# Hymba step on one core: four of the nine token-square sums as a multiply-and-sum on VectorE, their task spawned later

## The chip, the cores and the metric

The kernel runs on one core of a Trainium2 chip. The metric is the device time of one execution in microseconds (us), as the median of the runs shown. The names of the engines are those of the profile: PE is TensorE's matmuls, PEld its weight loads, DVE is VectorE, ACT is ScalarE, POOL is GpSimd, and SP is SyncE, which here only issues DMAs. A queue of DMA issues on an engine is written SPq or ACTq.

## The reference

One layer is computed for 1024 prompt tokens and 32 sample tokens (T = 1056 columns in all, model width 1024). Both branches read the same normalised input through one input projection; the outputs of both are gated and go through one output projection.

```python
def _rmsnorm(x, g):
    y = xf * lax.rsqrt(jnp.mean(xf * xf, axis=-1, keepdims=True) + EPS) * g
...
hn = _rmsnorm(x, ln_g)
q, k, v, ga, u, gs = jnp.split(hn @ w_in, [...])
att = stick_breaking(q, k, v)                 # 8 heads x 64, strictly causal
...
ab = exp(a * dt); bb = (ab - 1) / a * b       # complex, 32 groups x 64 states
h = scan(ab, bb @ u); y = gelu(c @ h + d_skip * u)
ssm_y = y * sigmoid(y @ w_glu + b_glu)
...
out = concat[_rmsnorm(att) * silu(ga), _rmsnorm(ssm_y) * silu(gs)] @ w_out
return x + out, k, v, h_last                  # then a last _rmsnorm
```

The mean of xf * xf over the 1024 columns of each token is what the change is about: nine blocks of up to 128 tokens, one sum per token.

## The kernel before, in words

**Products.** fp32 matrices are split into a high and a low part, and each product is made of three matmuls: high x high (`xh,w_hi`), low x high (`xl,w_hi`), high x low (`xh,w_lo`). I call these three a triple. ACT writes the high part of a weight (`w_hi`), DVE or POOL the low one (`w_lo`). The x that is multiplied is not yet normalised: the reciprocal root `rsc` of each token is worked out beside, spread over all partitions by PE (`tr<-ident,rsc`) and copied to `rsx`, by which every projected tile is scaled when it leaves PSUM.

**Order of the projections.** The 1056 tokens are cut into 256, 384 and 416. `slot(i, ...)` works through one group of 128 output columns in 24 steps (8 slices of the contraction x 3 cuts). Slot 0 makes two groups of u while the inputs arrive; then come the other groups of u, the gate groups (`gs`), the first attention gate (`ga`, stored as `tga_d`), q, k and v. PE's matmuls of the slots fill the time in which the state-space branch waits for other engines.

**The state-space branch.** `angles` and `params_d` make sines, cosines (tables `RT`), step parameters (`P`) and the powers of the step (`PW`); `s_mats(m)` makes from them the matrices `W` (written `W<-Pm,Bm`, `tW`), which PE transposes. u is stored scaled to DRAM (`ud`) and read back as `U`. `s_states(m)` runs the scans (`E<-dec,E`) on DVE, up to `bst`; `s_out(m)` makes Y on PE in two halves (`z<-U,Tm` and `z<-bst,V`) of which ACT takes the gelu out of PSUM, writes Y to DRAM (`yd`) and reads it back turned (`yj`). When all four m are there, ACT and DVE split y (`yh`, `yl`) and `glu` makes the products with `w_glu` (`z<-yh,wgh` and so on) for the three cuts. Behind the last of these `ssm_gate` loads the gate (`gs<-gs_d`), multiplies on DVE, takes its sigmoid on ACT (`sgs`) and multiplies on POOL (`y_nat<-y_nat,sgs`), for m = 0 to 3; two buffers hold the gates, so those of m = 2 and 3 are loaded when the first two are used up. The attention starts at the first `z<-kA,qA`.

**What sets the order.** Every call on an engine goes through the helper `Timed.call` (line 215, so that all rows of the profile bear this line). The helper keeps an estimated clock for each engine (class `Clock`, l. 72 to 150). `spawn` puts a task, a Python generator, on a list; `tick`, called at each step of a slot, goes on with each task whose data are ready by the estimated clock (`at`, `dve`) or that was named as done. An engine runs its instructions in the order in which they were so issued. A task that is issued elsewhere, or priced otherwise, therefore moves other tasks' instructions too.

**The square task.** `x_rs` (l. 386) takes the nine blocks in turn. Block 8 has 32 tokens and shares its buffer with block 0, so its load is issued once block 0 is squared. `x_sq` (l. 377) squares a block in place on ACT with the sum in `rst`; then come six small operations on POOL (`rsqrt`), the transposes on PE and the copies to `rsx`. The task is spawned at step `RSS % 24` of slot `RSS // 24`, `angles` and `params_d` at that of `PST`, which is 34 (slot 1, step 10).

Of the kernel before, what the change touches and what calls it, by code (L numbers as in the profile page):

```python
# [12 lines left out]
AF = mybir.ActivationFunctionType  # L13
OP = mybir.AluOpType
# [10 lines left out]
NCH = 133  # L25
NB = 134
NK = 25
RSS = 28
LEAD = 1
WARM = 9  # L30
WL = {1: ((1, slice(0, 1)),), 2: ((0, slice(1, 3)), (1, slice(1, 3))), 4: ((0, slice(3, 8)),), 5: ((1, slice(3, 8)),)}
# [188 lines left out]
def hymba_step(ctx, tc, xT, xn, w_in, ln_g, kcT, vc, w_glu, b_glu, w_out, g_att, g_ssm, final_g,  # L220
               prm, h0, bmat, cvec, cbd, dsk, consts_in,
               y_out, kT_out, vT_out, st_out):
    nc = Clock(tc.nc)
# [153 lines left out]
    def x_sq(b):  # L377

        m, _ = blk(b)
        nc.scalar.activation(xq[b][:m], xq[b][:m], AF.Square, accum_out=rst[:m, 1, b:b + 1])  # L380

    xq = {}
    rsc = const.tile([128, 9], F32, name="rsc")
    rst = const.tile([128, 2, 9], F32, name="rst")

    def x_rs():

        for b in range(9):
            if b == 1:
                x_load(8)  # L390
            yield at(xq[b], lead=300.0)
            x_sq(b)
        rsqrt(rsc, rst[:, 1], 1.0 / D, rst[:, 0], rst[:, 1])
        yield at(rsc)
        for i, (t0, n) in enumerate(TC):
            pb = p_tr()
            for b in range(t0 // 128, (t0 + n + 127) // 128):
                m, c = blk(b)
                nc.tensor.matmul(pb[:, c.start - t0:c.stop - t0], rsc[:m, b:b + 1].to_broadcast([m, 128]),
                                 ident[:m, :m], start=True, stop=True)  # L400
            act(rsx[:, t0:t0 + n], pb[:, :n])
            done.add(f"rs{i}")
            yield 3 if i == 0 else 1

    def blk(b):
        return min(128, T - 128 * b), slice(128 * b, min(T, 128 * b + 128))
# [336 lines left out]
    with ExitStack() as s1:  # L743
# [100 lines left out]
        def angles():  # L844

            u = ss.tile([128, 16, NK], F32, name="ang_u", tag="E")
            v = sa.tile([128, 16, NK], F32, name="ang_v", tag="W")
            sb = [128, 16, NK]
            kb = kidx[:, None, :].to_broadcast(sb)
            yield "pa"  # L850
            tt(v, kb, p8[:, :, None].to_broadcast(sb), OP.mult)
            yield dve()
            ts(v, v, MAGIC, MAGIC, OP.add, OP.subtract)
            yield dve()
            tt(u, kb, ph[:, :, None].to_broadcast(sb), OP.mult)
            yield dve()
            tt(u, u, v, OP.subtract)
            yield dve()
            tt(v, kb, pl[:, :, None].to_broadcast(sb), OP.mult)
            yield dve()  # L860
            tt(u, u, v, OP.add)
            yield dve()
            ts(u, u, 0.5, -0.5, OP.min, OP.max)
            yield dve()
            sincos(RT[:, 1], RT[:, 0], u, v)
            params_b()
            done.add("pb")
            yield 2
            params_c()
            done.add("pc")  # L870
# [279 lines left out]
        def at_step(slot, k, f, *a):  # L1150
            ev.setdefault((slot, k), []).append((f, a))
# [8 lines left out]

        at_step(RSS // 24, RSS % 24, spawn, x_rs())
        at_step(PST // 24, PST % 24, spawn, angles())
# [905 lines left out]
```

## Time and profile before

| | |
|---|---|
| median of 3 runs | 681.17 us (680.73 to 681.33) |
| the profiled execution | 682.8 us |
| its span in the trace | 680.9 us |
| mean granted clock of TensorE | 0.968 |
| PE busy | 626.7 us (92%) |
| DVE busy | 429.1 us (63%) |
| ACT busy | 346.3 us (51%) |
| POOL busy | 228.1 us (33%) |

The span is what the trace covers, from its first to its last instruction; the time of the execution is 1.9 us more. All times inside the kernel are us from the start of the span. A row of a timeline gives start, length, engine, operation, output and inputs, and in brackets the idle time before it with what ended it. [...]

### The profile page before, as it was taken

To read this page: it belongs to the slowest core of one execution; us is meant where nothing else is said; L and a number is where in the kernel's file an instruction comes from. 1 tells how busy PE (TensorE), PEld (TensorE's weight loads), DVE (VectorE), ACT (ScalarE), POOL (GpSimd) and SP (SyncE) were. 2 spreads that over 40 slices of the span, in tenths; PEclk is the share of its full clock that TensorE was granted. 3 is DMA by queue.
4 is the path that set the end of the run, shared out by engine and by line. 5 is a ranking of instruction groups with operands and counts; after the bars stand their busy time and mean duration, and the time that the engine had idled before them with its cause. 6 is when DMAs were issued, how large, how long until landed. Compare 5 with 4: busy or idle time off the path is not lost.

```text
span 680.9 us, 10474 instructions
## 1 busy us (share of the span) xinstructions
PE 626.7 (92%) x3760; PEld 523.9 (77%) x3760; DVE 429.1 (63%) x670; ACT 346.3 (51%) x787; POOL 228.1 (33%) x334
## 2 busy tenths in 40 slices
PE   7948999999969993899999999999998899997995
PEld 6938899988969993788878698886775566756873
DVE  5947999889335443465776565656557948364654
ACT  5572423252555643566766657555765645442332
POOL 0011122000122167444345343432417513133885
PEclk7969999999979996999999999999999999998999
DMA  8726342552520144210221112333162795218552
GB/s 307 270 90 175 95 143 79 178 167 66 177 69 24 56 166 153 67 36 25 64 87 59 46 44 74 95 103 102 39 184 92 254 286 178 69 63 269 182 172 100
DMA packets 64132, 83.46 MB, mean 123 GB/s; under 512 B 9040, under 2 KB 47248, under 8 KB 64080
## 3 DMA queue, kind: packets, MB, share of 16 engines
q1 hardware_dynamic: 57600, 71.23, 32.4%
q10 hardware_dynamic: 6480, 11.56, 5.4%
q8 instruction: 30, 0.49, 0.3%
q14 instruction: 22, 0.18, 0.1%
HBM read 56.29 MB, written 26.48 MB: 122 GB/s over the span
## 4 chain that ended last, share of the span: by engine, by line
PE 69%; POOL 6%; DMA 5%; ACT 4%; issue 3%; DVE 3%; SPq 1%; DVEq 0%; POOLq 0%; ACTq 0%
PE pj L215 36%; PE z L215 14%; PE pv L215 10%; PE tr L215 8%; POOL rst L215 2%; DMA gs<-gs_d 1%; DMA x<-in_xn 1%; POOL rsA L215 1%; DMA w_raw<-in_w_in 1%; DMA yj<-yd 1%; DVE cb L215 1%; DMA yd<-Y 1%; SPq L215 1%; POOL s__6538 L215 0%; DMA O<-att_d 0%
## 5 line engine op out<-in xcount | busy, mean ns | idle before, releaser
L215 PE MATMUL pj<-xh,w_hi 128*128 128x256 f32 (+2 forms) x472 | 163.9, 350 | 0.0
L215 PE MATMUL pj<-xl,w_hi 128*128 128x256 f32 (+2 forms) x472 | 151.4, 324 | 0.0
L215 PE MATMUL pj<-xh,w_lo 128*128 128x256 f32 (+2 forms) x472 | 151.3, 323 | 0.0
L215 PEld LDWEIGHTS pj<-xh,w_hi 128*128 128x128 f32 x472 | 89.9, 190 | 23.7 <-issue 19.8
L215 DVE TENSOR_TENSOR_SCAN cb<-cb,own 128x896 f32<-128x896 f32 (+3 forms) x64 | 96.5, 1514 | 15.0 <-ACT cb L215 12.8
L215 PEld LDWEIGHTS pj<-xl,w_hi 128*128 128x128 f32 x472 | 90.2, 191 | 1.7
L215 PEld LDWEIGHTS pj<-xh,w_lo 128*128 128x128 f32 x472 | 89.5, 190 | 0.3
L215 ACT ACTIVATE cb<-z 128x512 f32<-128x512 f32 (+4 forms) x102 | 49.8, 488 | 53.0 <-PE z L215 34.7
L215 PE MATMUL pj<-xh,S 128*128 128x512 f32 (+3 forms) x212 | 69.4, 405 | 2.1 <-DVE x L215 1.5
L215 POOL TENSOR_TENSOR betaL<-betaL,cb 128x896 f32<-128x896 f32 (+2 forms) x24 | 41.4, 1725 | 60.8 <-DVE cb L215 36.9
L215 POOL TENSOR_TENSOR w_lo<-w_raw,w_hi 128x512 fp32r<-128x512 f32 x30 | 46.5, 1550 | 44.3 <-ACT w_hi L215 44.3
L215 ACT ACTIVATE wt<-tr 128x512 f32<-128x512 f32 (+2 forms) x86 | 47.2, 552 | 16.6 <-PE tr L215 16.3
L215 PE MATMUL pv<-wt,vS 128*64 128x256 f32 x320 | 52.0, 404 | 1.1 <-POOL wt L215 1.1
L215 POOL TENSOR_TENSOR betaS<-betaS,cb 128x128 f32<-128x128 f32 (+3 forms) x32 | 27.1, 851 | 73.2 <-DVE cb L215 38.3
L215 PEld LDWEIGHTS pj<-xh,S 128*128 128x128 f32 (+2 forms) x212 | 36.2, 184 | 17.2 <-issue 7.5
L215 DVE TENSOR_TENSOR kv_out<-pj,rsx 128x256 f32<-128x256 f32 (+2 forms) x55 | 28.3, 514 | 29.5 <-PE pj L215 29.0
L215 PE MATMUL pj<-xl,S 128*128 128x512 f32 (+3 forms) x112 | 43.1, 387 | 0.0
L215 ACT ACTIVATE w_hi<-w_raw 128x512 fp32r<-128x512 f32 x44 | 27.6, 630 | 27.0 <-DMA w_raw<-in_w_in 17.0
L215 PE MATMUL tr<-ident,betaL 128*128 128x128 f32 x226 | 35.8, 276 | 4.1 <-ACT wt L215 2.6
L215 ACT ACTIVATE betaL<-z 128x512 f32<-128x512 f32 (+4 forms) x70 | 35.8, 512 | 0.0
L215 PEld LDWEIGHTS tr<-ident,betaL 128*128 128x128 f32 x226 | 26.9, 141 | 11.1 <-ACT wt L215 3.4
L215 DVE TENSOR_TENSOR attT<-pv,attT 64x256 f32<-64x256 f32 x32 | 13.4, 420 | 32.6 <-ACT attT L215 32.4
(273 smaller groups left out, 1273.3 us busy)
## 6 DMA issues: line engine op xcount, KB each, us to landing
w_raw<-in_w_in ACTq DMA_DIRECT2D x44, 256.0 KB, 2.6
xq<-in_xn SPq DMA_DIRECT2D x8, 512.0 KB, 7.4
x<-in_xn SPq DMA_DIRECT2D x8, 512.0 KB, 5.7
yp_d<-x SPq DMA_DIRECT2D x8, 512.0 KB, 2.9
x<-yp_d SPq DMA_DIRECT2D x8, 512.0 KB, 5.2
y_out<-x SPq DMA_DIRECT2D x8, 512.0 KB, 2.9
xr<-in_xT SPq DMA_DIRECT2D x7, 528.0 KB, 8.6
wraw<-in_w_out SPq DMA_DIRECT2D x5, 512.0 KB, 5.3
```

Source lines behind the costliest of these rows:

```text
L215: return g(*args, **kw)
```

## The change

```diff
-RSS = 28
+SQD = (1, 3, 5, 7)
+RSS = 40
...
     def x_sq(b):
 
         m, _ = blk(b)
-        nc.scalar.activation(xq[b][:m], xq[b][:m], AF.Square, accum_out=rst[:m, 1, b:b + 1])
+        s_ = rst[:m, 1, b:b + 1]
+        if b in SQD:
+            nc.vector.tensor_tensor_reduce(xq[b][:m], xq[b][:m], xq[b][:m], 1.0, 0.0, OP.mult, OP.add, accum_out=s_)
+        else:
+            nc.scalar.activation(xq[b][:m], xq[b][:m], AF.Square, accum_out=s_)
```

Blocks 1, 3, 5 and 7 are multiplied by themselves and summed on DVE, in one instruction each and a second that writes the sum out; blocks 0, 2, 4, 6 and 8 stay on ACT. The task is spawned at slot 1, step 16 and no more at slot 1, step 4, which puts it behind the tasks of the sines and of the step parameters. All other code is the same, but the tasks are issued anew by the estimated clock. Three places of the order follow.

**First place, ACT, behind the last split of x (`xh<-xr`) and its two weight loads.** `RT` are the tables, `P` the step parameters, `uj` copies of the first projections out of PSUM. Before:

```order
L215 ACTIVATE xq,rst<-xq 128x1024 x8
L215 ACTIVATE xq,rst<-xq 32x1024
L215 ACT_TABLE_LOAD
L215 ACTIVATE RT<-ang_u 128x400
L215 ACTIVATE RT<-ang_v,hpi 128x400
L215 ACTIVATE P<-P 128x16
L215 ACTIVATE P<-P,hpi 128x16
L215 ACTIVATE uj<-z 128x8x32
L215 ACTIVATE uj<-z 128x8x48
L215 ACTIVATE uj<-pv 128x8x48
L215 ACTIVATE uj<-pv 128x8x4
L215 ACTIVATE w_hi<-w_raw 128x512 x2
```

After the change:

```order
L216 ACT_TABLE_LOAD
L216 ACTIVATE RT<-ang_u 128x400
L216 ACTIVATE RT<-ang_v,hpi 128x400
L216 ACTIVATE P<-P 128x16
L216 ACTIVATE P<-P,hpi 128x16
L216 ACTIVATE xq,rst<-xq 128x1024 x4
L216 ACTIVATE uj<-z 128x8x32
L216 ACTIVATE uj<-z 128x8x48
L216 ACTIVATE uj<-pv 128x8x48
L216 ACTIVATE uj<-pv 128x8x4
L216 ACTIVATE w_hi<-w_raw 128x512 x2
L216 DMA w_raw<-in_w_in 128x512
```

Eight 1024-wide squares and the 32-token one stood ahead of the table load and the sines; four stand behind them now, and the 32-token one has gone further down, behind four more `uj` copies.

**First place, DVE, behind the step parameters `P`; the ISA rows are the new sums, `bb` is a coefficient, `PW` the powers.** Before:

```order
L215 TENSOR_TENSOR P<-P 128x16 x4
L215 TENSOR_TENSOR bb<-bm,P 128x256
L215 TENSOR_TENSOR w_lo<-w_raw,w_hi 128x512
L215 TENSOR_TENSOR PW<-PW 128x16
L215 TENSOR_TENSOR t_485<-PW 128x16
L215 TENSOR_TENSOR PW<-PW,t_485 128x16
```

After the change:

```order
L216 TENSOR_TENSOR bb<-bm,P 128x256
L216 ISA xq,rst<-xq 128x1024
L216 ISA rst 128x1
L216 ISA xq,rst<-xq 128x1024
L216 ISA rst 128x1
L216 ISA xq,rst<-xq 128x1024
L216 ISA rst 128x1
L216 ISA xq,rst<-xq 128x1024
L216 ISA rst 128x1
L216 TENSOR_TENSOR w_lo<-w_raw,w_hi 128x512
L216 TENSOR_TENSOR PW<-PW 128x16
L216 TENSOR_TENSOR t_478<-PW 128x16
```

Four sums stand between `bb` and the low part of the weight.

**Second place, PE, at the last `s_out` (m = 3), whose products are the rows with `z`.** Before:

```order
L215 MATMUL z<-U,Tm 128x133 x2
L215 MATMUL z<-bst,V 128x133 x4
L215 MATMUL z<-U,Tm 128x133 x2
L215 MATMUL z<-bst,V 128x133 x4
L215 MATMUL pj<-xh,w_hi 128x416
L215 MATMUL pj<-xl,w_hi 128x416
L215 MATMUL pj<-xh,w_lo 128x416
L215 MATMUL z<-U,Tm 128x133 x2
L215 MATMUL z<-bst,V 128x133 x4
L215 MATMUL z<-U,Tm 128x133 x2
L215 MATMUL z<-bst,V 128x133 x4
L215 MATMUL pj<-xh,w_hi 128x416
```

Behind this there were 14 more triples, 15 with the one that begins in the last row, up to the first `z<-yh,wgh`. After the change:

```order
L216 MATMUL z<-U,Tm 128x133 x2
L216 MATMUL z<-bst,V 128x133 x4
L216 MATMUL z<-U,Tm 128x133 x2
L216 MATMUL z<-bst,V 128x133 x4
L216 MATMUL z<-U,Tm 128x133 x2
L216 MATMUL z<-bst,V 128x133 x4
L216 MATMUL z<-U,Tm 128x133 x2
L216 MATMUL z<-bst,V 128x133 x4
L216 MATMUL pj<-xh,w_hi 128x256
L216 MATMUL pj<-xl,w_hi 128x256
L216 MATMUL pj<-xh,w_lo 128x256
L216 MATMUL pj<-xh,w_hi 128x256
```

The triple between the two halves is gone, the halves are adjacent, and behind them stand 33 triples (16 of 256, 8 and 1 of 384 and 8 of 416 columns; before, 5 of 416, 8 of 256 and 2 of 384). On SP's queue the last read `yj<-yd` now stands behind `tga_d<-kv_out 128x256`; it stood directly behind a weight load.

**Third place, ACT, behind the last sigmoids of `glu`.** `sgs` is the sigmoid of the state-space gate, `vS` the transposed v. Before:

```order
L215 ACTIVATE w_hi<-w_raw 128x512
L215 DMA w_raw<-in_w_in 128x512
L215 ACTIVATE w_hi<-w_raw 128x512
L215 ACTIVATE vS_1875<-tr 128x256
L215 ACTIVATE sgs<-gs 128x1056
L215 DMA w_raw<-in_w_in 128x512
L215 ACTIVATE vS_1875<-tr 128x384
L215 ACTIVATE sgs<-gs 128x1056 x3
```

After the change:

```order
L216 ACTIVATE w_hi<-w_raw 128x512
L216 DMA w_raw<-in_w_in 128x512
L216 ACTIVATE sgs<-gs 128x1056
L216 ACTIVATE w_hi<-w_raw 128x512
L216 ACTIVATE vS_1870<-tr 128x256
L216 DMA w_raw<-in_w_in 128x512
L216 ACTIVATE sgs<-gs 128x1056
L216 ACTIVATE vS_1870<-tr 128x384
```

The first `sgs` stood behind the second `w_hi` and the first `vS`, and stands ahead of both. On POOL the first `y_nat<-y_nat,sgs` correspondingly stands ahead of the second `w_lo` of this stretch. From the first `z<-kA,qA` on, the order is the same on every engine.

## Rows read from the trace of the kernel before

**Rows 1.** The waits of PE: us in total, times, longest.

```profile
PE z L215 <- ACT w_hi L215: 11.6, 2, 9.8
...
PE tr L215 <- DVE W L215: 1.8, 1, 1.8
```

**Rows 2.** The timeline of ACT: start, length, operation, idle before.

```profile
35.01 1.06 ACT L215 ACTIVATE xq<-xq 128x1024 f32<-128x1024 f32 x1
...
36.28 1.06 ACT L215 ACTIVATE xq<-xq 128x1024 f32<-128x1024 f32 x1
...
42.56 0.29 ACT L215 ACTIVATE P<-P,hpi 128x16 f32<-128x16 f32 x1
...
43.98 1.17 ACT L215 ACTIVATE w_hi<-w_raw 128x512 fp32r<-128x512 f32 x2
```

**Rows 3.** The timeline of DVE, 32 to 60 us and at the last `bst`.

```profile
33.39 0.11 DVE L215 SCALAR_TENSOR_TENSOR P<-P 128x16 f32<-128x16 f32 x1
42.88 0.27 DVE L215 TENSOR_TENSOR PW<-P 128x16 f32<-128x16 f32 x2 [9.39 <-ACT P L215]
...
44.66 0.69 DVE L215 TENSOR_TENSOR w_lo<-w_raw,w_hi 128x512 fp32r<-128x512 f32 x1
...
48.11 0.68 DVE L215 TENSOR_TENSOR w_lo<-w_raw,w_hi 128x512 fp32r<-128x512 f32 x1
...
59.73 0.66 DVE L215 TENSOR_TENSOR uj<-z,rsx 128x256 f32<-128x256 f32 x1 [4.21 <-DMA ud<-uj]
...
171.66 1.34 DVE L215 TENSOR_TENSOR bst<-bst,st_t 128x536 f32<-128x536 f32 x2
```

**Rows 4.** DVE by form up to 200 us: busy, mean ns of one, idle.

```profile
L215 DVE TENSOR_TENSOR_SCAN E<-dec,E 128x536 f32<-128x536 f32 x8 | 10.0, 1265 | 0.4
...
L215 DVE SCALAR_TENSOR_TENSOR xl<-xr,lng,xh 128x1056 fp32r<-128x1056 f32 x7 | 9.2, 1314 | 1.7 <-ACT xh L215 1.7
...
L215 DVE TENSOR_TENSOR W<-W,tW 128x1024 f32<-128x1024 f32 x4 | 4.9, 1226 | 0.1
```

**Rows 5.** The timeline of PE at two restarts and behind the last state products.

```profile
44.68 0.58 PE L215 MATMUL z<-xh,w_hi 128*128 128x256 f32 x1 [9.80 <-ACT w_hi L215]
...
45.79 0.63 PE L215 MATMUL tr<-ident,rsc 128*128 128x128 f32 x2
...
182.76 0.45 PE L215 MATMUL pj<-xh,w_hi 128*128 128x416 f32 x1
...
194.78 0.58 PE L215 MATMUL z<-yh,wgh 128*128 128x256 f32 x1 [5.02 <-ACT yh L215]
```

**Rows 6.** Two windows: busy of PE, PEld, DVE, ACT, POOL; PE clock.

```profile
60.00:173.00 113.00, 110.54 (x779) 100.74 (x778) 103.98 (x130) 38.35 (x109) 13.83 (x26) 1.00 0.42 129
194.70:207.00 12.30, 11.54 (x69) 11.24 (x70) 4.25 (x7) 4.72 (x12) 5.16 (x6) 0.79 0.07 22
```

**Rows 7.** The chain that ended last, 150 to 200 us.

```profile
179.43 3.40 PE z L215 x24
...
183.56 3.92 DMA yd<-Y
...
194.76 1.24 DVE yl L215
```

**Rows 8.** Timelines of DVE, ACT, POOL, SP and PE ahead of the attention.

```profile
245.61 1.71 DVE L215 SCALAR_TENSOR_TENSOR y_nat<-y_nat,gssm,gs 128x1056 f32<-128x1056 f32 x1 [1.89 <-DMA gs<-gs_d]
...
247.72 0.63 ACT L215 ACTIVATE w_hi<-w_raw 128x512 fp32r<-128x512 f32 x1 [3.45 <-DMA w_raw<-in_w_in]
...
248.53 1.08 ACT L215 ACTIVATE sgs<-gs 128x1056 f32<-128x1056 f32 x1
...
250.63 4.86 POOL L215 TENSOR_TENSOR y_nat<-y_nat,sgs 128x1056 f32<-128x1056 f32 x2
...
254.01 0.72 SPq L215 DMA_DIRECT2D gs<-gs_d  x1
...
268.33 0.80 PE L215 MATMUL z<-kA,qA 128*128 128x512 f32 x1 [10.37 <-ACT betaL L215]
```


## The prediction

> **What bounds the kernel now.** I read the waits of PE first. PE is busy 92% of the span, so a saving counts only where PE waits, and the list says where: 9.8 us for a `w_hi` of ACT, 1.8 us for `W` of DVE [rows 1], 5.0 us for `yh` ahead of glu [rows 5], 10.4 us ahead of the attention [rows 8]. Then I read the timelines of ACT and DVE at the first wait, and see one chain. ACT squares block after block, a new one each 1.27 us (35.01, 36.28), and comes to the sines only behind them. DVE, which has finished the parameters `P` at 33.50, stands idle for 9.39 us until ACT's `P<-P,hpi` ends at 42.85. ACT's `w_hi`, for which PE waits, begins at 43.98, and PE goes on at 44.68 [rows 2, 3, 5]. Next come the windows: from 60 to 173 DVE is busy 103.98 of 113 us, so the engine that receives the four sums has little idle time, and its results (`W`, `bst`) are what PE takes next [rows 6]. Last, the chain that ended last shows what is behind the 5.0 us: from the end of the last `z` at 182.83 to the end of `yl` at 196.00 there are 13.2 us, two DMA flights among them [rows 7].
>
> **Part 1, the squares on ACT.** Nothing stands now between the parameters and the sines. DVE's `P` ends at 33.50, two short ACT operations follow (0.29 us for one, about 0.4 for both), and DVE can start on `PW` at 33.9 instead of 42.88, 9.0 us earlier. ACT then makes four squares, 4 x 1.27 = 5.1 us, to 39.0; the `uj` copies take what they took (42.88 to 43.98, 1.1 us), `w_hi` begins at 40.1 and PE, 0.7 us behind it as before, at 40.8 instead of 44.68: **-3.9 us** [rows 2, 3, 5]. The 32-token square and the six POOL operations come later, but `rsx` is first used by the scaling on DVE, which has moved behind `W`; that covers them. Without the cover, each us that `rsx` is late is a us of `uj`.
>
> **Part 2, the sums on DVE.** The trace of before has no multiply with a sum on DVE, so I bound it. Below: a plain product of two fp32 tiles of the same 1024 columns takes 1226 ns (1.20 ns a column), and one with a scalar 1314 ns for 1056 (1.24). Above: the slowest form, the scan, takes 1265 ns for 536 columns, 2.36 a column or 2.42 us for 1024 [rows 4]. The sum has the product's operands, so I take 1.28 us with its second, one-column instruction, and keep 2.42 for a rival. Four are 5.1 us. From `PW` to the `w_lo` there were 1.8 us (42.88 to 44.66); so DVE comes to the sums at 35.7 and to `w_lo` at 40.8, and ends it at 41.5, 0.7 us after PE's restart, as before (45.35 against 44.68) [rows 3, 5]. The second `w_lo` comes 3.45 us behind the first (44.66, 48.11) in either order, but the transposes `tr<-ident,rsc` that filled PE's time in between (0.63 us for two) are now behind it, so PE is earlier by about that: **+0.6 us** [rows 3, 5].
>
> [...]
>
> **Part 3, W.** The order has put `W` ahead of the scaling of `uj`. DVE starts this work at 33.9, 9.0 us earlier, and loses 5.1 of it to the sums; in front of `W` it also no longer does the scaling nor waits the 4.21 us for `ud` [rows 3]. `W` is then ready at least 9.0 - 5.1 + 4.2 = 8.1 us earlier, PE arrives 3.9 - 0.6 = 3.3 us earlier, and the wait goes: **-1.8 us** [rows 1]. What is late next is `ud` and `U`, since the scaling comes behind `W`; PE has the gate groups to work on meanwhile.
>
> **Part 4, the last states.** The last `bst` is done at 173.00 [rows 3]. If DVE kept all its idle time it would be done 9.0 - 5.1 = 3.9 us earlier, at 169.1. The 4.21 us for `ud` are filled by `W`: 164.9. Of the 9.0 idle us in the window (113.0 - 103.98) another 4.8 may go, since PE and ACT deliver earlier: 160.1 [rows 3, 6]. PE wants `bst` at about 163.3 (worked out in part 5). I take a stall of **+0.5 us**, near the low end, since PE's deliveries move by 5 us too; the high end, 5.8, is a rival.
>
> **Part 5, the wait ahead of glu.** In the order after, the halves of the last `s_out` are adjacent, so PE waits once for ACT to empty the bank (from 182.83 to 183.56 [rows 7]): **+0.7 us**. Without any wait of its own PE would come to `z<-yh` at 194.78 - 3.9 + 0.6 - 1.8 + 0.7 - 5.0 = 185.4. Before, 15 triples with 4896 columns took 182.76 to 189.76 [rows 5], 1.43 ns for a column of a triple. Now 33 with 10,880 columns follow: 15.6 us. So the last `z` ends at 169.8, its two halves (3.4 each [rows 7]) start at 162.3, and `bst` is wanted about a us later. The chain of 13.2 us then ends at 183.0, plus what SP's queue adds: the read `yj` now stands behind a `tga_d` that waits for a sigmoid on ACT. I bound that by nothing and by one more flight of 3.92 us [rows 7] and take 2: 185.0, or 186.9 at worst, against 186.0, where PE wants `yl`. Of the wait, 5.0 and the 0.7 us in which `yl` was late (195.36 to 196.00 [rows 5, 7]), 0.5 is left: **-5.2 us**.
>
> **Part 6, the clock.** Behind this wait the granted clock is 0.79 of full speed in the 12.3 us up to 207, where PE is busy nearly throughout [rows 6]: 12.3 x 0.21 = 2.6 us lost. The shorter wait for `W`, 1.8 us, lies in the window from 60 us on, whose clock is 1.00 [rows 1, 6]. With 0.5 us of idling I expect no fall: **-2.6 us**. If it fell all the same, nothing is gained here.
>
> **Part 7, ahead of the attention.** There `sgs` starts at 248.53 because it stands behind a `w_hi` that waited 3.45 us for its weight; the gate that it reads had landed by 245.61, when DVE began with it. POOL's product starts at 250.63, behind a `w_lo` of that same weight [rows 8]. In the order after, both stand ahead: the product starts once DVE's product ends, at 245.61 + 1.71 = 247.3, 3.3 us earlier. SP issues the last gate load (254.01) behind the store of that product, so it moves along, and with it the chain up to the attention's first product, before which PE waits 10.4 us: **-3.3 us**. From there on the order is unchanged, and I count nothing.
>
> **Sum.** -3.9 + 0.6 - 1.8 + 0.5 + 0.7 - 5.2 - 2.6 - 3.3 = -15.0. The profiled execution took 682.8 us, so 667.8; the median of the runs is 1.6 lower, so I forecast **666.2 us**, by its own unknowns 661 to 670: all plus terms at nothing and no wait left give 663.9, and I allow 3 us for the tail; without the clock's 2.6 and with 1.2 us of wait it is 669.5.
>
> **Rivals.**
> - *The sum runs at half speed.* 2.42 us each by the scan's row, 4.6 us more on DVE ahead of `w_lo`, for which PE then stands: 671. For it: the form is not in the trace; against it: two fp32 sources alone cost nothing extra [rows 4]. [...]
> - *DVE becomes the bound.* It sheds no idle time and `bst` is done at 169.1: PE stands 5.8 us at the last `s_out`, the clock falls behind that wait, and 2.6 us are not won: 666.2 + 5.3 + 2.6 = 674. For it: 92% busy [rows 6]; against it: 4.21 us of idle are filled by name in the new order.
> - *The wait only moves.* Glu comes sooner, but its wait, its clock and the tail stay: only parts 1 to 3 count, -5.1, so 676.
> - *No change within 0.2%.* The waits that stay eat parts 1 to 3 too.
> - *Slower.* One mechanism: the custom sum is much dearer than any DVE row. It lies on the way to `w_lo`, so each us counts four times; at 1.28 + 15.0 / 4 = 5.0 us for one, the gain is gone, and at 7 us the kernel is at 689. For it: no row shows the form; against it: no DVE row needs over 2.4 ns a column.
>
> **Chances.** The forecast 0.56; half speed 0.12; DVE the bound 0.14; the wait only moves 0.06; no change 0.04; slower 0.08. So faster by over 0.2% (1.4 us, about what a measurement of this kernel can tell from no change) 0.88, within it 0.04, slower 0.08. The range 661 to 677 takes in the first four cases, less some of their edges.
>
> **What would show it.** Part 1: PE's first long wait ends near 40.8, DVE's idle behind `P` is under 1 us. Part 2: the sums last 1.2 to 1.3 us each, at 35.7 to 40.8. Part 3: no wait for `W`. Part 4: PE's wait for `bst` under 1 us. Part 5: the wait for `yh` and `yl` under 1.5 us together. Part 6: the clock at 1.00 in the first 12 us of glu. Part 7: the first POOL product 3.3 us earlier against the end of glu. A sum over 2 us, a wait of several us for `bst`, or a tail of the old length would make the forecast wrong.

## The result

The changed kernel takes 675.92 us (median of 4 runs, 675.37 to 677.25), the kernel before 681.25 beside it: a ratio of 0.9922, interval 0.9903 to 0.9942. The forecast was 666.2 us in a range of 661 to 677; it had the sign right and the gain of 5.3 us nearly three times too large. Two later measurements of the same file gave 0.9947 (0.9925 to 0.9970) and 0.9904 (0.9873 to 0.9936); single executions over the three lay between 673.9 and 681.1 us. The profiled execution took 675.9 us with a span of 674.1, so the traces differ by 6.8 us of span, of which 1.6 lie in the profiled execution of before, which was that much over its median.

The waits of PE in the changed kernel, those that matter here (us in total, times, longest):

```profile
PE z L216 <- ACT w_hi L216: 5.1, 1, 5.1
PE tr L216 <- DMA U<-ud: 3.9, 2, 3.5
...
PE pj L216 <- DVE kv_out L216: 2.8, 1, 2.8
...
PE z L216 <- ACT Y L216: 0.5, 1, 0.5
```

Against [rows 1, 5, 8] the reader is to see: the wait for `w_hi` fell from 9.8 to 5.1 us, those for `W`, `yh` and `yl` are gone, and two that were not there have come: 3.9 us for `U`, which a DMA brings, and 2.8 us for a `kv_out` of DVE. The timeline of PE at these places:

```profile
38.24 0.58 PE L216 MATMUL z<-xh,w_hi 128*128 128x256 f32 x1 [5.07 <-ACT w_hi L216]
...
39.26 0.58 PE L216 MATMUL z<-xh,w_lo 128*128 128x256 f32 x1 [0.22 <-DVE w_lo L216]
...
42.73 0.58 PE L216 MATMUL z<-xh,w_lo 128*128 128x256 f32 x1 [0.54 <-DVE w_lo L216]
...
71.01 1.16 PE L216 MATMUL tr<-U,WT 128*64 128x133 f32 x8 [3.54 <-DMA U<-ud]
...
191.33 0.44 PE L216 MATMUL pj<-xh,w_hi 128*128 128x384 f32 x1 [2.78 <-DVE kv_out L216]
...
235.17 0.35 PE L216 MATMUL z<-yh,wgl 128*128 128x416 f32 x1
...
260.61 0.79 PE L216 MATMUL z<-kA,qA 128*128 128x512 f32 x1 [7.93 <-ACT betaL L216]
```

The last product of glu in the kernel before:

```profile
241.48 0.35 PE L215 MATMUL z<-yh,wgl 128*128 128x416 f32 x1
```

PE restarts at 38.24 instead of 44.68, waits twice more for a `w_lo`, stands 3.54 us at 71.01, comes to `z<-yh` without a wait of its own at 191.97 (194.78 before) because the triple ahead of it waited 2.78 us, ends the last product of glu at 235.5 (241.8 before) and gets `betaL` at 260.61 (268.33). The first sum and the last on DVE, and what follows:

```profile
33.94 1.22 DVE L216 CUSTOM_DVE_ANT_0 xq<-xq 128x1024 f32<-128x1024 f32 x1
35.08 0.08 DVE L216 DVE_READ_ACCUMULATOR2_ANT rst<- 128x1 f32 x1
35.08 1.22 DVE L216 CUSTOM_DVE_ANT_0 xq<-xq 128x1024 f32<-128x1024 f32 x1
...
38.52 0.69 DVE L216 TENSOR_TENSOR w_lo<-w_raw,w_hi 128x512 fp32r<-128x512 f32 x1
```

A sum takes 1.22 us, the next starts 1.14 us later, and the second instruction lies within that; four take 4.6 us. The form does not run at half speed, which would be the rival's 2.42 us. On ACT the squares follow each other every 1.04 us now, not 1.27 as in [rows 2]:

```profile
32.17 1.04 ACT L216 ACTIVATE xq<-xq 128x1024 f32<-128x1024 f32 x1
...
33.21 1.04 ACT L216 ACTIVATE xq<-xq 128x1024 f32<-128x1024 f32 x1
```

The granted clock, in windows of the changed kernel (busy of PE, PEld, DVE, ACT and POOL, then the clock as a share of full speed, DMA share, GB/s), then in two of the kernel before that were not shown yet, then behind the wait ahead of glu in the last of the three profiles of the changed kernel:

```profile
36.85:38.24 1.39, 0.00 (x0) 0.00 (x1) 1.39 (x3) 1.39 (x5) 0.00 (x0) 0.50 0.00 0
38.24:46.84 8.60, 7.84 (x30) 7.25 (x31) 7.80 (x29) 5.46 (x20) 4.49 (x7) 0.50 0.20 62
60.00:75.00 15.00, 11.46 (x72) 9.94 (x70) 14.90 (x19) 3.87 (x16) 3.56 (x8) 0.89 0.85 201
191.90:204.20 12.30, 12.30 (x86) 12.27 (x85) 5.55 (x11) 7.14 (x15) 4.77 (x5) 1.00 0.15 51
```

```profile
39.50:44.68 5.18, 0.00 (x0) 0.00 (x1) 1.66 (x13) 5.13 (x13) 2.96 (x8) 0.50 0.01 2
44.68:49.68 5.00, 5.00 (x22) 4.78 (x23) 4.79 (x22) 1.98 (x6) 0.00 (x0) 0.50 0.17 52
```

```profile
191.90:204.20 12.30, 12.26 (x76) 12.25 (x77) 4.00 (x9) 5.58 (x12) 4.00 (x4) 0.86 0.10 39
```

After its first long wait PE ran 5.0 us at a granted clock of 0.50 (half clock) before the change and 8.6 us after it. The clock had fallen while PE still waited, 5.2 us before the restart in the kernel before and 1.4 us in the changed one; in both it was low for 10.2 us in all (39.5 to 49.7 and 36.8 to 47.1), and behind the shorter wait more of that falls on work. Around the wait for `U` the clock fell too: 0.89 of full speed from 60 to 75, where [rows 6] have 1.00. Behind the wait ahead of glu, which is now 2.78 us for `kv_out`, it stays at 1.00 in this execution, where it was 0.79; in the last profile of the changed kernel, behind 2.86 us, it is 0.86.

### The profile page after: what moved, and what is told of

The parts are those of the page before. It is cut to its first block, busy times and chain, and to the rows that moved or that the text cites. A ratio compares the mean times of both kernels' runs of the same rounds, so it can differ in the third digit from the quotient of the medians.

```text
span 674.1 us, 10469 instructions
## 1 busy us (share of the span) xinstructions
PE 629.6 (93%) x3760; PEld 524.5 (78%) x3760; DVE 435.3 (65%) x678; ACT 340.7 (51%) x777; POOL 230.3 (34%) x334
## 5 line engine op out<-in xcount | busy, mean ns | idle before, releaser
L216 DVE TENSOR_TENSOR_SCAN cb<-cb,own 128x896 f32<-128x896 f32 (+3 forms) x64 | 95.0, 1490 | 15.3 <-ACT cb L216 13.3
L216 PEld LDWEIGHTS tr<-ident,betaL 128*128 128x128 f32 x226 | 27.3, 142 | 10.2 <-ACT wt L216 3.4
```

Source lines behind the costliest of these rows:

```text
L216: return g(*args, **kw)
```

## The experiments

Where it says "it leaves the order", every engine's instructions stand as in the changed kernel but for those moved or added: the planner's clock is told the old engine and place, so nothing else shifts.

**The two parts of the change alone.** First the later spawn only:

```diff
-SQD = (1, 3, 5, 7)
+SQD = ()
 RSS = 40
```

> Only the later spawn, all nine sums on ACT. The order of the instructions is that of the changed kernel on every engine, but for the sums themselves. Theory A (the four sums are worth what they take off ACT ahead of w_hi, and DVE has the room): four more squares of 1.04 us stand on ACT ahead of w_hi, so PE's first long wait ends about 4.2 us later than in the changed kernel (38.2 to 42.4), W and U follow by about as much, and the time is 679 to 680.5 us. Theory B (DVE is the bound up to glu, so what ACT gains DVE loses): the wait for w_hi is longer, a later wait is shorter by as much, and the time stays within 1 us of 675.9.

Measured: 1.0008 of before (0.9984 to 1.0032), no change. The order is that of the changed kernel, with eight squares on ACT instead of four. PE restarts at 43.70, stands 3.42 us for `U` and 2.88 us for `kv_out`:

```profile
43.70 0.58 PE L216 MATMUL z<-xh,w_hi 128*128 128x256 f32 x1 [9.45 <-ACT w_hi L216]
...
75.79 1.15 PE L216 MATMUL tr<-U,WT 128*64 128x133 f32 x8 [3.42 <-DMA U<-ud]
...
197.11 0.44 PE L216 MATMUL pj<-xh,w_hi 128*128 128x384 f32 x1 [2.88 <-DVE kv_out L216]
```

This is theory A in its direction, with 2.5 to 4 us more than it gave. It also says something that the forecast had not: the reordering, which the forecast's parts 3 to 7 credited with 11.7 us, gains nothing while the squares stay on ACT. What it takes off at `W`, ahead of glu and in the tail it puts on at `U`, at `kv_out` and in half clock. The gain comes with the four sums in this order, 0.992 against 1.001.

Then the sums only:

```diff
 SQD = (1, 3, 5, 7)
-RSS = 40
+RSS = 28
```

> Only the four sums on DVE, spawned where they were before. The order then puts the sines behind the copies of the first projections and behind two weights on ACT, and the scaling of uj ahead of PW on DVE; Tm stands behind U on SP again. Theory A: PE's first long wait ends early, near 38 us, U comes without a wait, but W is late, since the sines start some 10 us later than in the changed kernel; a wait for W of 2 to 6 us, and 673 to 679 us. Theory B (DVE is the bound): no better than before, 681.

Measured: 692.75 us, 1.0158 of before (1.0121 to 1.0195). Both theories missed it: the issue order puts the table load at 52 us and the first `RT` at 59.80, 29 us later than in the changed kernel, so that `W`, `bst`, `yh` and `yl` are all waited for. So in this order the sums do not pay: with the early spawn the planner puts the sines behind copies and weights, and the late spawn is needed with them.

**The price of a sum.** Each sum made twice, the second time into a column that nobody reads; it leaves the order:

```diff
             nc.vector.tensor_tensor_reduce(xq[b][:m], ..., accum_out=s_)
+            nc.vector._e.tensor_tensor_reduce(xq[b][:m], ..., accum_out=rsdup[:m])
...
```

> The changed kernel with each of the four sums on DVE made twice, the second time into a column that nobody reads; all else in the same order. Theory A (the sums lie on the way to w_lo, and each us of them is a us of PE): four more of 1.15 us make w_lo 4.6 us later, PE waits 4 to 5 us for it behind its first two products, and the time is 4 to 5 us over the changed kernel run beside it. Theory B (DVE's time there is covered by a later wait, the ones for U and kv_out): the wait for w_lo grows, those for U and kv_out shrink, and the time is less than 2 us over it.

Measured: 680.96 us, 0.9992 (0.9972 to 1.0011), against 0.9947 (0.9925 to 0.9970) for the changed kernel run beside it (the base, below):

```profile
44.85 0.58 PE L216 MATMUL z<-xh,w_lo 128*128 128x256 f32 x1 [5.29 <-DVE w_lo L216]
```

PE waits 5.29 us for `w_lo` where it waited 0.22, and the later waits (2.59 for `U`, 2.77 for `kv_out`) do not shrink. The span is 4.7 us longer than that of the first of the two base profiles, as theory A has it; by the ratios the difference is 0.45%, 3 us. The sums lie on the path, as forecast.

**U behind Tm.** One DMA issue moved on SP; it leaves the order:

```diff
             yield at(md[0:128], lead=500.0)
+            if m == 0:
+                yield "U1"
             nc.sync.dma_start(Tm, ...)
```

> The changed kernel with one DMA issue moved: the first Tm<-md behind the two U<-ud on SP, all else in the same order. Theory A (U was late since its issue stood behind a Tm that waited for its own store): U is issued when ud has landed, near 60.4 instead of 64.1, PE's wait of 3.5 us for U falls under 1 us, the granted clock between 60 and 75 us rises from 0.89 to near 1.00, and 3 to 5 us come off: 671 to 673 us. Theory B (U is late because of the DMA load in that stretch, or the wait only moves on to bst or to the chain ahead of glu): the wait for U stays over 2 us, or another wait grows by as much, and the time stays at 675 to 676.

SP's queue in the changed kernel, then in this one:

```profile
57.59 0.34 SPq L216 DMA_DIRECT2D md<-Ms  x1
...
63.66 0.37 SPq L216 DMA_DIRECT2D Tm<-md  x1
64.12 1.00 SPq L216 DMA_DIRECT2D U<-ud  x2
```

```profile
58.70 0.34 SPq L216 DMA_DIRECT2D md<-Ms  x1
...
61.42 4.21 SPq L216 DMA_DIRECT2D U<-ud  x2
65.69 0.45 SPq L216 DMA_DIRECT2D Tm<-md  x1
```

The first read of `U` is issued 2.7 us behind the issue of `md` instead of 6.5 us, because it no longer stands behind a `Tm` that waits for the store of `md`. PE's wait for the first `U` is gone, the clock from 60 to 75 is 1.00, and the time is 673.92 us, 0.9878 of before (0.9848 to 0.9908). PE's other waits show what was given back: 1.3 us for the next `W`, and 3.3 us for `kv_out`.

For the place this is theory A. Of the time 2 us come off against 675.92, less than the 3 to 5 expected, and the interval overlaps that of the lowest of the three ratios of the changed kernel (0.9873 to 0.9936), which was not run beside this one.

**The last yj behind the gate's store.** One DMA issue moved from SP to ACT's queue; it leaves the order:

```diff
-        put(dst[:, t0:t0 + n], sg[:, :n])
+        if i == 0 and EARLY and not ga_n:      # the first tga_d alone
+            later.append([PUT + 1, go])        # go: the same dma_start on nc.scalar
+        else:
+            put(dst[:, t0:t0 + n], sg[:, :n])
```

> The changed kernel with one DMA issue moved: the first store of the attention gate, tga_d 128x256, from SP to ACT's queue, so that the last yj<-yd is no longer behind it; all else in the same order. Theory A (that queue place makes yl late, and through the PSUM copy that stands behind yl on DVE it makes PE wait 2.8 us ahead of glu): yj is issued about 2.5 us earlier, near 178.7, the wait of PE falls under 1 us, and 1.5 to 2.8 us come off: 673 to 674.5. Theory B (the chain of flights itself is too long): the wait stays over 2 us and the time at 675 to 676.

SP's queue in the changed kernel, then in this one, with the `y_nat` on ACT that reads `yj`:

```profile
174.62 0.33 SPq L216 DMA_DIRECT2D yd<-Y  x1
180.92 0.32 SPq L216 DMA_DIRECT2D tga_d<-kv_out  x1
181.29 0.43 SPq L216 DMA_DIRECT2D yj<-yd  x1
```

```profile
171.29 0.33 SPq L216 DMA_DIRECT2D yd<-Y  x1
174.00 0.37 SPq L216 DMA_DIRECT2D yj<-yd  x1
...
179.17 0.63 ACT L216 ACTIVATE w_hi<-w_raw 128x512 fp32r<-128x512 f32 x1 [2.08 <-DMA w_raw<-in_w_in]
...
180.14 2.33 ACT L216 ACTIVATE y_nat<-yj 128x1024 f32<-128x1024 f32 x2
```

`yj` is issued 2.7 us behind `yd` instead of 6.7: the queue had cost 4.0 us. But PE's wait for `kv_out` falls by 1.3 us only, to 1.49. `yj` has landed by 178.0 (4.0 us of flight) and ACT starts `y_nat` at 180.14, because a `w_hi` stands ahead of it that waits 2.08 us for its weight. The time is 672.34 us, 0.9870 (0.9837 to 0.9904). That is more than this wait can give; in this execution the wait for `U`, which the edit does not touch, was 1.43 us without a fall of the clock. In the changed kernel it was 3.54, 2.21 and 2.52 us in three profiles, each time with a fall. Nor is a fall of the clock seen behind the wait for `kv_out` here: ACT starts the first three sigmoids of glu 2.66, 4.79 and 7.27 us behind the end of that copy, against 2.66, 4.81 and 7.29 in the first profile of the changed kernel, where the clock was 1.00. So how much of the gain is the edit's, this run does not show; its interval too overlaps that of the lowest ratio of the changed kernel.

Both DMA moves together:

> Both DMA moves in one kernel: Tm behind U on SP, the first tga_d on ACT's queue. Theory A (two separate waits): the wait for U is under 1 us and the one for kv_out under 1.6 us, and the time is 4 to 6 us under the changed kernel run beside it, 669 to 672. Theory B (the wait only moves): the two together give no more than the better of them alone, some 3 us.

Measured: 671.63 us, 0.9840 (0.9807 to 0.9873). No wait for the first `U`, 1.80 us for `kv_out`, and a new 1.89 us for the second `W`, with the clock at 0.50 for some 3 us behind it: a matmul of 416 columns took 0.54 to 0.69 us from 92.66 to 95.04, where it was 0.35 ahead of the wait. This is clear of the changed kernel run beside it (0.9925 to 0.9970). Both waits are shorter in one kernel, as theory A has it, with part of the gain turned into the wait for `W`; but against the better of the two single moves (0.9870) the difference lies within the intervals, so the times do not show that the gains add up.

**The half clock behind the restart.** The second `w_lo` made by POOL instead of DVE; it leaves the order:

```diff
-        tt(l, raw_t.pop(ci), h, OP.subtract, eng or nc.gpsimd)
+        r = raw_t.pop(ci)                      # ci == 5: on POOL, else as before
+        if ci == 5:
...
+            nc.gpsimd._e.tensor_tensor(l, r, h, OP.subtract)
...
```

> The changed kernel with the second low part of a weight behind the sums (w_lo of 128x512) on POOL, which is idle there, instead of DVE; the order of all else is kept. After its restart PE ran 8.6 us at half clock in the changed kernel and 5.0 before, and in the changed kernel it waited once more for this w_lo, 0.54 us, 4.5 us behind the restart. Theory A (that short wait is what keeps the clock low, so its price is not 0.6 but some 2.3 us): the wait is gone, the half clock ends about 5 us behind the restart, and 2 to 2.5 us come off at that place; the wait for U may give some of it back, so 673 to 675 us against 675 to 678 of the changed kernel run beside it. Theory B (the clock stays low for another reason, such as the wait for w_hi being shorter): the wait is gone, the half clock still lasts over 7.5 us, and at most 0.6 us comes off.

```profile
40.01:46.31 6.30, 6.08 (x26) 5.79 (x27) 6.06 (x25) 3.96 (x12) 4.04 (x5) 0.51 0.12 43
60.00:75.00 15.00, 11.86 (x72) 10.33 (x71) 14.04 (x18) 3.97 (x16) 2.94 (x8) 0.84 0.96 215
```

The wait of 0.54 us is gone and the half clock lasts 6.3 us behind the restart instead of 8.6, which is theory A for that place; with all three moves (below) it is 6.4. The time, 677.04 us or 0.9930 (0.9903 to 0.9957), is no better than that of the changed kernel run beside it (0.9904, below): PE comes to `U` earlier, waits 3.14 us for it, and the clock from 60 to 75 is 0.84.

With `U` out of the way as well, all three moves in one kernel:

> Tm behind U on SP, the first tga_d on ACT's queue, and the second w_lo on POOL, in one kernel. Theory A (three separate losses): 2 us under the kernel with the two DMA moves, 668 to 670.5 us, 0.981 to 0.985 of before. Theory B (what is gained ahead of W turns into a wait for W or for bst): no better than with the two DMA moves, 671 to 672.

```profile
PE tr L216 <- DVE W L216: 2.1, 1, 2.1
...
PE pj L216 <- DVE kv_out L216: 1.7, 1, 1.7
```

Measured: 670.57 us, 0.9828 (0.9793 to 0.9863), the fastest that was run. No wait for the first `U` is left, and `W` and `kv_out` are what PE still waits for. It is clear of the changed kernel run beside it (0.9873 to 0.9936). Against the kernel with two moves the difference lies within the intervals, so that the third adds anything is not shown by the times.

**The tail.** The last two gate products on DVE instead of POOL; it leaves the order:

```diff
-                tt(yv, yv, sg, OP.mult, gp)
+                if m < 2:
+                    tt(yv, yv, sg, OP.mult, gp)
+                else:
...
+                    nc.vector._e.tensor_tensor(yv, yv, sg, OP.mult)
```

> The changed kernel with the last two of the four gate products y_nat<-y_nat,sgs on DVE instead of POOL; the order of all else is kept. Theory A (the tail was 3.3 us forecast and 1.4 measured because DVE's product y_nat<-y_nat,gssm,gs, 1.3 us before, took 2.6 and 3.4 us beside a POOL product, and because the rsqrt on POOL queues behind the last gate product): the last such DVE product takes 1.3 to 1.5 us, the rsqrt on POOL starts about 2.5 us sooner after the end of glu, and 2 to 3 us come off. Theory B (the tail is bound by the landing of the last gate load): the rsqrt starts less than 1 us sooner and the time is within 1 us of the changed kernel's.

The tail of the changed kernel on POOL and DVE, then the last products in its second profile, then DVE's last product in the kernel before, then the places in this one:

```profile
239.99 2.31 POOL L216 TENSOR_TENSOR w_lo<-w_raw,w_hi 128x512 fp32r<-128x512 f32 x1
242.26 2.48 POOL L216 TENSOR_TENSOR y_nat<-y_nat,sgs 128x1056 f32<-128x1056 f32 x1
...
246.98 5.88 POOL L216 TENSOR_TENSOR y_nat<-y_nat,sgs 128x1056 f32<-128x1056 f32 x2
254.11 2.41 POOL L216 TENSOR_TENSOR y_nat<-y_nat,sgs 128x1056 f32<-128x1056 f32 x1 [1.26 <-DVE rsc L216]
256.60 0.20 POOL L216 TENSOR_SCALAR rst<-rsc 128x9 f32<-128x9 f32 x1
...
242.95 5.19 DVE L216 SCALAR_TENSOR_TENSOR y_nat<-y_nat,gssm,gs 128x1056 f32<-128x1056 f32 x2
...
250.59 3.38 DVE L216 SCALAR_TENSOR_TENSOR y_nat<-y_nat,gssm,gs 128x1056 f32<-128x1056 f32 x1 [1.96 <-DMA gs<-gs_d]
```

```profile
247.80 9.22 POOL L216 TENSOR_TENSOR y_nat<-y_nat,sgs 128x1056 f32<-128x1056 f32 x3
...
250.79 1.58 DVE L216 SCALAR_TENSOR_TENSOR y_nat<-y_nat,gssm,gs 128x1056 f32<-128x1056 f32 x1 [1.33 <-DMA gs<-gs_d]
```

```profile
260.39 1.32 DVE L215 SCALAR_TENSOR_TENSOR y_nat<-y_nat,gssm,gs 128x1056 f32<-128x1056 f32 x1 [3.79 <-DMA gs<-gs_d]
```

```profile
235.83 0.35 PE L216 MATMUL z<-yh,wgl 128*128 128x416 f32 x1
...
248.91 3.28 DVE L1277 TENSOR_TENSOR y_nat<-y_nat,sgs 128x1056 f32<-128x1056 f32 x1
...
254.02 1.26 DVE L1277 TENSOR_TENSOR y_nat<-y_nat,sgs 128x1056 f32<-128x1056 f32 x1
...
255.71 0.20 POOL L216 TENSOR_SCALAR rst<-rsc 128x9 f32<-128x9 f32 x1 [4.64 <-DVE rsc L216]
```

Measured: 675.97 us, 0.9916 (0.9892 to 0.9941). The changed kernel run beside it took 678.40 us, 0.9947 (0.9925 to 0.9970); the intervals overlap, so that this is faster is not shown. Counted from the end of glu (235.5 and here 236.2), the rsqrt starts 19.5 us later, where it was 21.1 (20.8 in the two other profiles of the changed kernel): 1.2 to 1.6 us sooner, between the two theories. DVE's last `gssm` product takes 1.30 us here, as theory A had it; it only starts at 252.61, since the gate product ahead of it took 3.28 us beside one on POOL (1.26 us for the last, which ran alone), and PE waits 3.02 us for a `kv_out` that DVE reaches later. Part of what POOL no longer does, DVE now does late.

**The base.** The changed kernel was run once more in each of two further measurements: beside the doubled sums, both DMA moves and the gate on DVE, and beside the moved `w_lo` and the three moves:

> The changed kernel once more, beside the three others, as their base. Every theory: 675 to 677 us, a ratio to before near 0.992, the wait for U 1 to 4 us and the one for kv_out 2 to 3 us.

> The changed kernel once more, beside the two others, as their base: 675 to 678 us.

Measured: 678.40 us (0.9947) and 675.50 us (0.9904); the waits for `U` were 2.21 and 2.52 us, those for `kv_out` 1.63 and 2.86.

## Why the prediction was wrong

- **Part 1, -3.9 us: right in mechanism, too small.** The restart came 6.4 us earlier. Before, nine squares stood ahead of the sines; now none does. Of the 2.5 us over the forecast 1.6 are a start that was later in the profiled execution of before (PE fell idle at 34.9 there, at 33.2 after; it lies between 32.9 and 35.4 over all traces): `PW` came 10.6 us earlier instead of 9.0, and counted from DVE's `P` that is the forecast. The other 0.9 are the four squares, 1.04 us each instead of 1.27.
- **Part 2, +0.6 us: the term was mis-sized.** The price of a sum was right (1.14 instead of 1.28) and PE's waits for `w_lo` came to 0.8. What was left out is the half clock, which lasted 8.6 us instead of 5.0: another 3.6 x 0.5 = 1.8 us. Of this 2.3 x 0.5 = 1.2 hang on the second wait, as moving that `w_lo` showed. The rest goes with the shorter wait: the clock had fallen 5.2 us before the restart in the kernel before and 1.4 us before it here, so more of the low stretch falls on work. That is read from the windows; no run was made for it.
- **Part 3, -1.8 us: the step that failed.** `W` came in time. The prediction named `ud` and `U` as late next and then let them pass: "PE has the gate groups to work on meanwhile". It had not counted SP's queue, on which the new order puts the store of `md`, two loads and `Tm` ahead of `U`. PE stood 3.9 us for two `U`, and the clock at 0.89 over 15 us cost 1.65 more. The experiment with that one issue moved removes the wait and the low clock, though later waits take back part of the time.
- **Part 4, +0.5 us: nothing.** PE waited for no `bst`; the rival in which DVE becomes the bound at the last states did not come.
- **Part 5, -5.2 us: half right.** The wait ahead of glu fell from 5.7 to 2.8 (1.6 and 2.9 in the two other profiles). Adjacent halves cost 0.5, as forecast 0.7. The queue cost 4.0 us, where the bound was 3.92 and 2 was taken, and the consumer was not `yl` but the copy `kv_out` that DVE makes behind it, for which a triple ahead of `z<-yh` waits.
- **Part 6, -2.6 us: right in this execution, by luck.** The forecast's reason was a wait of 0.5 us; PE waited 2.78 us, and the clock stayed at 1.00 all the same. In four other profiles, one of them of the changed kernel, it fell to 0.50 at a wait of 2.77 to 2.92 us in this place.
- **Part 7, -3.3 us: mis-sized, 1.4.** From the last product of glu to `betaL` it is 25.1 us (235.5 to 260.6) where it was 26.5 (241.8 to 268.3). `sgs` came early, as forecast, but POOL became the bound: from 239.99 to 252.86 it has no gap, each `w_lo` takes 2.3 us and a product 2.5 to 2.9. In this execution it starts the last at 254.11, once DVE's product at 250.59 is done, which took 3.38 us beside it; alone it was 1.32 in the kernel before. In the second profile DVE's product takes 1.58 us, and instead POOL's last three take 3.1 each without a gap; alone one took 2.41. The forecast took the products' times as if the other engine were idle. Where the two engines' products ran at the same time they were longer: on DVE 3.4 us in the first profile against 1.3 alone, on POOL 3.1 as the mean of three in the second, part of them beside DVE, against 2.4 alone. Why, no run shows.
- **From the attention on, 0: +0.9.** 413.5 us instead of 412.6, with the same order. From 518 the clock was at 0.50 for 6.8 us, where in the kernel before, from 527, it was so for 3.4; that would cover it, but no run was made for it.

The terms as measured: -6.4 + 0.8 + 1.8 - 1.8 + 3.9 + 1.65 + 0.5 - 2.9 - 2.6 - 1.4 + 0.9 = -5.6, and 0.6 for a wait for `bst` of before that is gone as well, so -6.2 of the -6.8 between the spans; 0.6 us is not accounted for. The rival "the wait only moves" at 676 gave the measured time, but by luck: it counted parts 1 to 3 in full and left the wait ahead of glu, its clock and the tail as they were, while here part 3 was lost at `U` and some of parts 5 to 7 was won. That waits move is what it had right: with the spawn alone they cancel to 1.0008.

## What to carry to other kernels

When an edit moves a step ahead, follow the data of the step that it overtakes through every in-order queue, the DMA issue queue first: an issue that must wait for a store holds back all that stand behind it, here some 4 us at two places, though the data of those were there. A short wait right behind a restart (here 0.54 us, with 2.3 us more at half clock), or a few us of waiting in full flow (3.54 us for `U`, with 3.4 at half clock), is to be priced with the clock that may follow it, not by its own length alone; and as the same wait costs the clock in one execution and not in the next (at `kv_out`, 2.77 and 2.78 us), one trace of each kernel is not enough to price it. And where a planner reorders, time the reordering alone: here it gained nothing until work had also been taken off the engine that PE waits for.

## What the runs showed of the hardware

Behind the first long wait the granted clock stayed at 0.50 for 5.0 us when PE did not wait again (the kernel before), 6.3 us with one further wait of 0.22 us (the second `w_lo` on POOL), and 8.6 us with waits of 0.22 and 0.54 us (the first profile of the changed kernel); with the sums alone, one wait of 0.85 us, 1.3 us behind the restart, went with 6.0. Waits for `U` of 3.54, 2.21, 2.52 and 2.29 us at full clock were followed by 3 to 4 us at 0.50 (in the changed kernel three times and in the one with the gate on DVE), those of 3.42 (the spawn alone) and 3.14 us (`w_lo` on POOL) by some 6; one of 2.59 us with the sums made twice, and one of 1.43 with the last `yj` moved, were not. At the wait for `kv_out` the clock fell in four profiles: for 3.4 to 3.5 us with waits of 2.84 (the gate on DVE), 2.86 (the third profile of the changed kernel) and 2.92 us (`w_lo` on POOL), and for 5.9 us with one of 2.77 (the sums made twice). There a matmul of 256 columns took 0.41 us, where it takes 0.28 at full clock. In the first profile of the changed kernel, with 2.78 us, it did not fall. The same wait does not always cost the clock. A multiply with a sum on DVE, two fp32 sources of 128x1024, took 1.22 us, no more than the plain product in [rows 4].
